# Hybrid-mixer decoder on one core: dense row products joined from 256 to 512 weight columns

## The chip, the cores and the metric

The kernel runs on 1 core of one Trainium2 chip. The metric is the device time of the whole program in microseconds; three runs of the kernel before gave 2924.04, 2924.26 and 2918.29 us, median 2924.04.

## The reference, cut to what matters

Two layers, each over 16 learned tokens, 2048 prompt tokens and 8 single-token samples. Four head groups (HGRN2, gated DeltaNet, Mamba-2 SSD, retention) read columns of one input projection; their gated outputs are joined and go through the output projection.

```python
proj = einsum('btd,de->bte', rms_norm(h, norm_w[l]), w_in[l])      # D_MODEL 1024 -> 4108 columns
...
s_ret, o_d = run_mixer(chunk_scalar_decay, step_scalar_decay,
    (rotary(to_heads(d_q, 4), pos), rotary(to_heads(d_k, 4), pos) * QK_SCALE, to_heads(d_v, 4), ret_g), s_ret, prompt)
y_d = group_norm(from_heads(o_d), ret_norm_w_l, ret_norm_b_l, 4) * silu(d_z)
y = concatenate([y_a, y_b, y_c, y_d], -1)
h = h + einsum('bte,ed->btd', y, w_out[l])                          # 1024 -> 1024
```

The retention queries d_q and keys d_k are 256 columns each, and stand next to each other in w_in (D_Q = 3084, D_K = 3340). Everything is float32.

## The kernel before, in words

**Tokens.** There are NT = 17 tiles: tile 0 has 40 rows (16 of padding, 16 learned tokens, 8 samples), the others 128 prompt tokens each. Two tiles make a block, and the first block has three (tiles 0, 1, 2); 8 blocks in all.

**Dense products in two parts.** Activations and weights are split into a high and a low fp32r part, and a product is the sum of three matmuls: high by high, high by low, low by high. There are two forms. `dense_cm` (L473 to L475) keeps weights stationary and streams a block's tokens, for a channel-major result. `dense_rows` (L483 to L485) keeps a tile's 128 (or 40) tokens stationary and streams weight columns, for a token-major result: for each of 8 slices d of the 1024 inputs three matmuls of 256 columns, 24 in a group that fills half a PSUM bank. The trace names what both read `xh`, `xl` (activations) and `wh`, `wl` (weights); the result is `pd`, a pool of two banks.

**Weights.** `wpiece` (L450 is its last line of work) loads 1024 numbers per partition (`wr`), casts them to the high part on ACT (L449, `wh`) and subtracts for the low part on DVE or POOL (L450, `wl`). A piece of `load_tm` is 4 slices of 256 columns, so a group of 256 columns needs 2 pieces. Parts lie in a ring of 6 slots and a second one of 2.

**Stages of a layer.** SSD, gated DeltaNet, HGRN2, retention (`mixD`), output projection (`outproj`). The recurrent walk of gated DeltaNet is cut into parts that `hook` lets out between pieces of the later stages, one for each unit of credit.

**mixD.** For each block: a group per tile for the queries, then one per tile for the keys, then values, then the gate in channel-major form. The eviction of a query or key group, `ev`, is the rotary: on DVE L1522 and L1524, L1525 read PSUM (256, 128 and 128 columns) and write `dt` tiles, L1526 adds; POOL multiplies by the decay (L1528). The `dt` tiles come from a ring of 4. After that each tile is transposed (L1544), scored (`sc<-dqk`), and its state is updated (L304).

**outproj.** For each tile: mixer rows `y` come back from DRAM as `yf` (L1604), ACT casts them to `xh` (L1606), DVE subtracts to `xl` (L1607); four groups of 256 columns follow, and each is added to the residual `hx` by DVE (L1613). In layer 0 the tile is then normalised and transposed (L507) for layer 1; in layer 1 it is normalised (L1623) and stored.

**Order.** A list scheduler with a timing model of its own lays out each engine's instructions from the traced program; on the chip each engine keeps that order. Evictions and weight loads are given priority (`early`, 3000 instructions ahead). Weight columns from the layer after are loaded by steps of a generator during the last tile of `outproj` (`between`).

Of the kernel before, what the change touches and what calls it, by code (L numbers as in the profile page):

```python
# [92 lines left out]
def body(tc, ctx, a, o, nch, depth, blks, off):  # L93
# [3 lines left out]
    BW = 296  # L97
# [35 lines left out]
    def later(f):  # L133
        """emit f after the next piece of work that is put off"""
        pend.append(f)
        while len(pend) > 1:
            pend.pop(0)()
# [7 lines left out]
    def hook(n=1):  # L145
        """the next parts of the walk that runs beside other work"""
        credit[0] += n
        while credit[0] >= 1:
            credit[0] -= 1
            if walk and next(walk[0], 0) == 0:  # L150
                walk.pop()

    @contextmanager
    def inorder(names):
        """what is emitted inside is issued after what was emitted before, on these engines"""
# [43 lines left out]
    def pair():  # L199
        """a bank per head half: row tiles of the array may not share a bank"""  # L200
        return psc.tile([128, 2, 512], F32, tag="sc", name="sc")
# [43 lines left out]
    # ---------------------------------------------------------------- constants  # L245
# [28 lines left out]
    # block-diagonal states (two heads a tile), in turns  # L274
# [4 lines left out]
    # full triangles (upper halves written), in turns; outside of their use: norm weights, retention's decay  # L279
# [8 lines left out]
    def next_state(L, m, pu, decay):  # L288
        """S = decay * S + update, block-diagonal"""
# [25 lines left out]
    # ---------------------------------------------------------------- helpers  # L315
# [4 lines left out]
    def power(dst, src, k=0):  # L320
        """src ** -0.5 (k=0) or 0.5 (k=1)"""
# [23 lines left out]
    def rms_scale(hx, R):  # L345
        """1 / rms of the rows"""
# [6 lines left out]
    # ---------------------------------------------------------------- per layer parameters  # L353
    def load_layer(l):
# [38 lines left out]
        # forget gate bounds: softmax of the logits over the depth axis, cumulative  # L393
# [34 lines left out]
    # ---------------------------------------------------------------- dense pieces  # L428
# [27 lines left out]
    def load_tm(w, cols, wide=False):  # L456
        n = sum(c[1] for c in cols)
        return [wpiece([w[512 * k:512 * k + 512, c0:c0 + cn] for c0, cn in cols], 4, n, wide) for k in range(2)]
# [20 lines left out]
    def dense_rows(ps, R, pcs, xh, xl):  # L479
        n = pcs[0][0].shape[2]  # L480
        for d in range(8):
            hi, lo = (x[:, d % 4] for x in pcs[d // 4])
# [12 lines left out]
    def xprep(L, t, hx, keep=False):  # L495
        """normalised rows of a token tile -> channel-major, in two exact parts, to DRAM or to the block's tiles"""
# [32 lines left out]
    def rowtile(b, nm):  # L529
        """token-major rows of 256 columns by tile"""  # L530
# [6 lines left out]
    def small(L, b, raw):  # L537
        """decays and step sizes from the narrow columns of a block's tiles"""
# [31 lines left out]
        # cumulative sums: ssd over the chunk, gdn over blocks of 32  # L570
# [15 lines left out]
    def group_scale(osrc, R, groups, eps):  # L586
        """rows scaled by 1 / rms of each group, in SBUF; eps: number or [R, groups]"""
# [26 lines left out]
    def finish(t, mi, osrc, R, eps, w, z, b=None):  # L614
        """group norm of the mixer rows; returns what takes them to channel-major, gate z [128, 2, R], and to DRAM"""
# [27 lines left out]
    # decode: partitions hold (head half, key), free (sample, pair, value)  # L643
# [12 lines left out]
    def dec_bcast(rows8):  # L656
        """[8, 256] rows -> [128 (hh k), (b p), 64]"""
# [8 lines left out]
    def pb(x, cols=None):  # L666
        """[128, 2, 8] channel-major sample columns -> [128, 8, 2, 64] broadcast over values"""
# [8 lines left out]
    def dec_sum(src, lhs, m):  # L676
        """sum over the key partitions"""
# [18 lines left out]
    # ---------------------------------------------------------------- HGRN2  # L696
# [4 lines left out]
    def mixA(L, W, b):  # L701
# [26 lines left out]
        for c0, Lc, tl in groups:  # L728
# [7 lines left out]
            def scores(h, w):  # L736
                """products of keys at j and queries at j + w in steps of h"""
# [127 lines left out]
    # ---------------------------------------------------------------- short convolutions  # L865
    def conv(L, ws, b, wi, key, hasb, out):
        """out: 3 tiles [128, 2, BW] (pairs of channel tiles)"""
# [53 lines left out]
    def conv_samples(L, wi, key, hasb, src, dst):  # L921
        """the taps come from the stored rows"""
# [29 lines left out]
    # ---------------------------------------------------------------- gated delta  # L952
# [17 lines left out]
    def prepB(L, bs):  # L970
        """what the blocks need before the states: inverses of the unit triangles"""
# [4 lines left out]
        # sums of squares of q per token and head  # L976
# [30 lines left out]
        def factors(j0, j1):  # L1007
            """factors of tiles j0 .. j1 from the sums of squares of their keys"""
# [21 lines left out]
        def scv(x, n0, n):  # L1030
            """blocks n0 .. n0 + n as [(block, row), head, column]"""
            return x[:, n0:n0 + n].rearrange("h n j i -> (n j) h i")

        # decay within blocks of 32
# [13 lines left out]
        def scores(b, t, pv, start):  # L1048
            """pv [rows, x, y, p, i]: keys by keys, keys by queries"""
# [45 lines left out]
        # negated inverse of the unit triangular blocks above the diagonal: even rows of a block in one partition,  # L1095
        # odd rows in another, each beside the whole block as it was
# [23 lines left out]
    def loadB(L, P, i):  # L1120
        """what a tile keeps in DRAM: q, k, v, inverses, scores; gates"""
# [9 lines left out]
        # a group's first tile may have to wait for the inverses  # L1131
# [6 lines left out]
    def keysB(L, X):  # L1138
        """a tile's operands for the walk over its blocks, in parts"""
# [15 lines left out]
        # running decay of a block, broadcast over key channels  # L1155
# [8 lines left out]
        # keys and queries of a block side by side, in turns  # L1164
# [23 lines left out]
    def stepB(L, X, bb):  # L1188
        """one block of the walk"""
# [17 lines left out]
    def walkB(L):  # L1207
        """the tiles in turn, in parts; a tile's operands are made during the one before"""
# [65 lines left out]
    def decB(L, ys, epsq):  # L1274
# [5 lines left out]
        # rows of v, keys scaled to unit length  # L1280
# [505 lines left out]
```

## Time and profile before

| what | value |
|---|---|
| median of 3 runs | 2924.04 us |
| lowest and highest | 2918.29 and 2924.26 us |
| span of the profiled execution | 2924.2 us |
| PE matmul, busy share of the span | 96% |
| DVE, ACT, POOL, busy share | 58%, 35%, 36% |
| mean granted TensorE clock | 0.984 |
| HBM traffic over the span | 118 GB/s |

The profiled execution's own time is its span, 2924.2 us, which is within 0.2 us of the median of the runs. Busy times of PE overlap, since matmuls are pipelined: one of 256 columns is listed with nearly 0.3 us, though the next starts far earlier. So the pace of a run of matmuls is read from the starts in the timeline, not from the mean of a group. A source line in the tables is a line of the kernel before. An idle time in brackets, with an arrow, is what the engine waited before that instruction and for whom.

### The profile page before, as it was taken

Reading aid. Unit: us, or ns where it says so; the run is one execution under the profiler, and the core shown is the slowest. Engines: PE = TensorE matmul, PEld = TensorE weight load, DVE = VectorE, ACT = ScalarE, POOL = GpSimd, SP = SyncE. Lnnn points to the kernel's source line nnn. Section 1 sums busy time; section 2 is a strip of 40 time slices with the busy share of each in tenths; the row PEclk is TensorE's granted clock in tenths of the full one; section 3 lists DMA queues with packets and bytes.
Section 4 is the critical chain, followed back from the end, with each engine's and each line's share of the span. In section 5 each row is a group of like instructions: output and inputs, shape, how many; then the busy total and the mean of one; then the engine's idle time right before and its main releaser. Section 6 shows DMA issues by size and latency. Waiting matters only on the chain.

```text
span 2924.2 us, 76217 instructions
## 1 busy us (share of the span) xinstructions
PE 2811.0 (96%) x31196; PEld 2631.0 (90%) x31196; DVE 1694.9 (58%) x4822; ACT 1010.7 (35%) x2547; POOL 1045.4 (36%) x2000
## 2 busy tenths in 40 slices
PE   6989999999999999999999999899999999999998
PEld 6889898988888899999999999888988888999998
DVE  6777765646566745364456767565556657445433
ACT  5545522333333412232244454133333333222221
POOL 4453555665232211110033543745742222112000
PEclk9999999999999999999999999999999999999999
DMA  7243364462231432247762433645432222331433
GB/s 181 68 151 118 127 163 122 133 188 76 63 112 60 129 95 88 74 128 212 215 204 93 127 106 103 152 128 152 139 101 69 78 99 83 96 116 63 134 131 109
DMA packets 391332, 349.92 MB, mean 120 GB/s; under 512 B 144312, under 2 KB 361904, under 8 KB 380744
## 3 DMA queue, kind: packets, MB, share of 16 engines
q1 hardware_dynamic: 387464, 335.96, 37.5%
q0 software_dynamic: 3520, 9.09, 1.5%
q8 instruction: 247, 4.05, 0.6%
q14 instruction: 101, 0.83, 0.1%
HBM read 247.06 MB, written 98.10 MB: 118 GB/s over the span
## 4 chain that ended last, share of the span: by engine, by line
PE 84%; DVE 6%; DMA 4%; POOL 3%; ACT 2%; issue 2%; SPq 0%; POOLq 0%; ACTq 0%; DVEq 0%
PE pd L473 10%; PE pd L474 10%; PE pd L483 10%; PE pd L484 10%; PE pd L475 10%; PE pd L485 10%; PE tr L235 7%; PE sc L235 5%; PE wo L235 5%; PE o L235 3%; DMA wr<-in_w_in_dram 1%; PE tr L611 1%; PE tr L507 1%; DVE hx L502 1%; POOL bR L1110 1%
## 5 line engine op out<-in xcount | busy, mean ns | idle before, releaser
L473 PE MATMUL pd<-xh,wh 128*128 128x256 f32 (+1 forms) x2816 | 832.1, 296 | 12.6 <-DVE hB L901 3.3
L474 PE MATMUL pd<-xl,wh 128*128 128x256 f32 (+1 forms) x2816 | 817.9, 290 | 0.0
L475 PE MATMUL pd<-xh,wl 128*128 128x256 f32 (+1 forms) x2816 | 814.1, 289 | 0.0
L483 PE MATMUL pd<-wh,xh 128*128 128x256 f32 (+3 forms) x2448 | 702.0, 287 | 6.4 <-DVE sraw L1342 4.6
L484 PE MATMUL pd<-wl,xh 128*128 128x256 f32 (+3 forms) x2448 | 700.8, 286 | 2.5 <-POOL wl L450 2.5
L485 PE MATMUL pd<-wh,xl 128*128 128x256 f32 (+3 forms) x2448 | 698.0, 285 | 0.2
L473 PEld LDWEIGHTS pd<-xh,wh 128*128 128x128 f32 x2816 | 543.9, 193 | 37.2 <-issue 16.8
L474 PEld LDWEIGHTS pd<-xl,wh 128*128 128x128 f32 x2816 | 543.8, 193 | 9.1 <-issue 6.6
L475 PEld LDWEIGHTS pd<-xh,wl 128*128 128x128 f32 x2816 | 543.6, 193 | 4.1 <-issue 2.6
L483 PEld LDWEIGHTS pd<-wh,xh 128*128 128x128 f32 (+1 forms) x2448 | 455.7, 186 | 12.6 <-issue 5.4
L484 PEld LDWEIGHTS pd<-wl,xh 128*128 128x128 f32 (+1 forms) x2448 | 455.8, 186 | 9.0 <-issue 3.4
L485 PEld LDWEIGHTS pd<-wh,xl 128*128 128x128 f32 (+1 forms) x2448 | 455.7, 186 | 4.4 <-issue 2.1
L304 DVE TENSOR_TENSOR sbd<-low,tr 64x128 f32<-64x128 f32 x384 | 109.0, 284 | 131.8 <-PE tr L235 113.4
L600 POOL TENSOR_SCALAR fm<-fm 128x4 f32<-128x4 f32 (+3 forms) x102 | 23.7, 233 | 419.2 <-DVE fm L597 393.1
L1613 DVE TENSOR_TENSOR hx<-hx,pd 128x256 f32<-128x256 f32 (+1 forms) x136 | 57.1, 420 | 175.5 <-PE pd L485 175.2
L327 POOL TENSOR_TENSOR fm<-fm,expo 128x4 f32<-128x4 f32 (+3 forms) x136 | 129.3, 951 | 49.0 <-DVE fm L602 38.7
L331 POOL TENSOR_SCALAR rm<-rm 128x1 f32<-128x1 f32 (+1 forms) x51 | 13.7, 269 | 367.2 <-ACT junk L349 366.3
L520 ACT ACTIVATE th<-pd 128x256 f32<-128x256 f32 (+2 forms) x162 | 62.3, 384 | 231.8 <-PE pd L475 194.9
L235 PEld LDWEIGHTS sc<-aq,ak 64*32 64x32 f32 (+1 forms) x7008 | 97.0, 108 | 39.7 <-issue 16.9
L235 PE MATMUL sc<-aq,ak 64*32 64x32 f32 (+1 forms) x7008 | 129.1, 200 | 2.5 <-ACT sq L773 2.0
L1110 POOL TENSOR_TENSOR bR<-bR,bW 128x120 f32<-128x120 f32 (+14 forms) x300 | 119.6, 399 | 21.6
L1109 POOL TENSOR_TENSOR bW<-bU,bR 128x120 f32<-128x120 f32 (+14 forms) x300 | 112.6, 375 | 36.4 <-DMA bR<-bscr 15.4
(519 smaller groups left out, 4989.0 us busy)
## 6 DMA issues: line engine op xcount, KB each, us to landing
xh<-xh SPq DMA_DIRECT2D x56, 1024.0 KB
xl<-xl SPq DMA_DIRECT2D x56, 1024.0 KB
wr<-in_w_in_dram SPq DMA_DIRECT2D x64, 512.0 KB
hx<-in_x_prompt_dram SPq DMA_DIRECT2D x32, 512.0 KB
y<-y SPq DMA_DIRECT2D x128, 128.0 KB
yf<-y SPq DMA_DIRECT2D x32, 512.0 KB
bld<-qkv SPq DMA_DIRECT2D x32, 384.0 KB
xh<-xh SPq DMA_DIRECT2D x8, 1184.0 KB
```

The lines of the kernel that those rows point to most:

```text
L235: T.matmul(out, l, r, start=start, stop=stop, skip_group_check=True)
L304: tt(new[rr, :, hh], low[rr, :, hh], pv, ALU.add)
L327: G.tensor_tensor(dst, src, e.broadcast_to(list(src.shape)), ALU.pow)
L473: T.matmul(ps, hi[:, d], b.xh[:, d, 0:b.n], start=(d == 0), stop=False)
L474: T.matmul(ps, hi[:, d], b.xl[:, d, 0:b.n], start=False, stop=False)
L475: T.matmul(ps, lo[:, d], b.xh[:, d, 0:b.n], start=False, stop=(d == 7))
L483: T.matmul(ps[0:R, 0:n], xh[:, d], hi, start=(d == 0), stop=False)
L484: T.matmul(ps[0:R, 0:n], xh[:, d], lo, start=False, stop=False)
L485: T.matmul(ps[0:R, 0:n], xl[:, d], hi, start=False, stop=(d == 7))
L520: act(th[0:R, 0:n], ps, AF.Tanh, scale=0.5)
L1109: f(wv, bcm(U_[0:2 * nu, j, j + 1:32], 1, m), bcl(R_[0:2 * nu, 0:m, j], 31 - j), ALU.mult)
L1110: f(R_[0:2 * nu, 0:m, j + 1:32], R_[0:2 * nu, 0:m, j + 1:32], wv, ALU.subtract)
```

## The change

Query and key columns of retention become one group of 512 columns per tile, and the output projection has two groups of 512 columns per tile in the place of four of 256. `load_tm` makes pieces of 2 slices by 512 columns (still 1024 numbers per partition), so a group needs 4 pieces and the number of pieces stays. The rotary runs over the two halves of the joined group. `hook` is called once with two units of credit, where it was called twice with one. The generator of the next layer's weights is advanced twice after each of two groups, where it was once after each of four.

```diff
     def load_tm(w, cols, wide=False):
         n = sum(c[1] for c in cols)
-        return [wpiece([w[512 * k:512 * k + 512, c0:c0 + cn] for c0, cn in cols], 4, n, wide) for k in range(2)]
+        nd = 2 if n == 512 else 4
+        r = 128 * nd
+        return [wpiece([w[r * k:r * k + r, c0:c0 + cn] for c0, cn in cols], nd, n, wide and k < 2) for k in range(8 // nd)]
...
     def dense_rows(ps, R, pcs, xh, xl):
-        n = pcs[0][0].shape[2]
+        nd, n = pcs[0][0].shape[1:3]
         for d in range(8):
-            hi, lo = (x[:, d % 4] for x in pcs[d // 4])
+            hi, lo = (x[:, d % nd] for x in pcs[d // nd])
...
     def weightsD(w):
-        return ([load_tm(w, [(c, 256)]) for c in (D_Q, D_K, D_V)], [load_cm(w, D_Z + 128 * p, True) for p in range(2)])
+        return ([load_tm(w, [(D_Q, 512)]), load_tm(w, [(D_V, 256)])], [load_cm(w, D_Z + 128 * p, True) for p in range(2)])
...
-        for x in range(2):
-            def ev(t, ps):
-                R = rows(t)
-                rp = L.rope[0:R, t - 1] if t else rope0[0:R]
-                cs, sn = rp[:, 0:32], rp[:, 32:64]
+        def ev(t, ps2):
+            R = rows(t)
+            rp = L.rope[0:R, t - 1] if t else rope0[0:R]
+            cs, sn = rp[:, 0:32], rp[:, 32:64]
+            for x in range(2):
+                ps = ps2[:, 256 * x:256 * x + 256]
...
-            dense_tm(W[0][x], b, ev)
-            hook(rD)
-        dense_tm(W[0][2], b, lambda t, ps: S.copy(v[t][0:rows(t)], ps))
+        dense_tm(W[0][0], b, ev)
+        hook(2 * rD)
+        dense_tm(W[0][1], b, lambda t, ps: S.copy(v[t][0:rows(t)], ps))
...
-        for qd in range(4):
+        for qd in range(2):
             ps = dense_rows(ptile(pd, "pd"), R, W[qd], yh[:, :, 0:R], yl[:, :, 0:R])
-            cs = slice(256 * qd, 256 * qd + 256)
+            cs = slice(512 * qd, 512 * qd + 512)
             tt(hx[0:R, cs], hx[0:R, cs], ps, ALU.add)
             if between:
                 with early():
+                    next(between)
                     Wn = next(between)
...
-            W = [load_tm(a["w_out"][l], [(256 * qd, 256)], qd == 0) for qd in range(4)]
+            W = [load_tm(a["w_out"][l], [(512 * qd, 512)], qd == 0) for qd in range(2)]
```

PE has 24096 matmuls before and 21648 with the change. On every engine the order is the same up to the first group of retention queries in layer 0, and again from the start of layer 1 up to its first group of retention queries; between those points the scheduler has laid it out anew. Counted in PE's order from there, dense matmuls stand in 174 unbroken runs before and in 135 with the change (retention and output projection of layer 0: 71 and 33, then 56 and 18; of layer 1: 68 and 2, then 59 and 2).

PE, output projection of layer 0 in its steady part, around the transposes (`tr<-ident,hx`) of one tile's normalised rows; before:

```order
L484 MATMUL pd<-wl,xh 128x256
L507 MATMUL tr<-ident,hx 128x128 x4
L485 MATMUL pd<-wh,xl 128x256
L483 MATMUL pd<-wh,xh 128x256
L507 MATMUL tr<-ident,hx 128x128 x4
L484 MATMUL pd<-wl,xh 128x256
```

and with the change:

```order
L485 MATMUL pd<-wh,xh 128x512
L486 MATMUL pd<-wl,xh 128x512
L487 MATMUL pd<-wh,xl 128x512
L509 MATMUL tr<-ident,hx 128x128 x8
L485 MATMUL pd<-wh,xh 128x512
L486 MATMUL pd<-wl,xh 128x512
L487 MATMUL pd<-wh,xl 128x512
```

The eight transposes of a tile stand together, where two dense matmuls stood between the fours; and each dense matmul has twice the columns.

DVE, retention of layer 0, around the rotary of two groups (`dt<-pd,rope` reads PSUM); before:

```order
L1522 TENSOR_TENSOR dt_15590<-pd,rope 128x256
L1524 SCALAR_TENSOR_TENSOR dt_15591<-pd,rope 128x4x32
L1525 TENSOR_TENSOR dt_15591<-pd,rope 128x4x32
L1526 TENSOR_TENSOR dt_15590<-dt_15590,dt_15591 128x256
L1556 TENSOR_TENSOR css<-sc,sq_114 128x2x2x128
L304 TENSOR_TENSOR sbd_110<-low,tr 64x2x64 x2
L620 TENSOR_REDUCE fm<-o 128x4
L621 TENSOR_SCALAR fm<-fm 128x4
L623 TENSOR_TENSOR xc<-o,fm 128x256
L1522 TENSOR_TENSOR dt_15622<-pd,rope 128x256
```

and with the change:

```order
L1525 TENSOR_TENSOR dt_15522<-pd,rope 128x256
L1527 SCALAR_TENSOR_TENSOR dt_15523<-pd,rope 128x4x32
L1528 TENSOR_TENSOR dt_15523<-pd,rope 128x4x32
L1525 TENSOR_TENSOR dt_15529<-pd,rope 128x256
L1527 SCALAR_TENSOR_TENSOR dt_15530<-pd,rope 128x4x32
L1528 TENSOR_TENSOR dt_15530<-pd,rope 128x4x32
L1529 TENSOR_TENSOR dt_15522<-dt_15522,dt_15523 128x256
L1529 TENSOR_TENSOR dt_15529<-dt_15529,dt_15530 128x256
L1559 TENSOR_TENSOR css<-sc,sq_115 32x2x2x32
```

The eight operations of a tile's query and key halves stand back to back, six readers of PSUM first; the scores' masking (`css`) and the state (`sbd`) come behind all of them, where they stood between two groups of four.

## Rows read from the trace of the kernel before

**Rows 1.** The page: busy times, and shares of the chain that ended last.

```profile
PE 2811.0 (96%) x31196; PEld 2631.0 (90%) x31196; DVE 1694.9 (58%) x4822; ACT 1010.7 (35%) x2547; POOL 1045.4 (36%) x2000
...
PE 84%; DVE 6%; DMA 4%; POOL 3%; ACT 2%; issue 2%; SPq 0%; POOLq 0%; ACTq 0%; DVEq 0%
```

**Rows 2.** Windows: us; busy us (count) of PE, PEld, DVE, ACT, POOL; clock; DMA.

```profile
1012.00:1276.00 264.00, 262.18 (x2593) 248.55 (x2591) 131.73 (x380) 64.85 (x158) 47.88 (x85) 1.00 0.27 87
1276.00:1488.00 212.00, 212.00 (x1795) 210.92 (x1794) 95.36 (x166) 56.67 (x91) 23.56 (x42) 1.00 0.69 208
2490.00:2735.00 245.00, 243.28 (x2123) 231.89 (x2122) 120.13 (x330) 64.07 (x149) 42.96 (x67) 1.00 0.30 97
2735.00:2918.00 183.00, 181.53 (x1521) 181.33 (x1519) 64.57 (x99) 32.60 (x48) 12.93 (x32) 1.00 0.37 125
```

**Rows 3.** Line L483 of dense_rows: count, duration ns (min/median/max), first and last start, forms.

```profile
L483 PE MATMUL pd<-wh,xh x2448: 274/283/573, 14.8 to 2916.0; 128*128 128x256 f32 x157, 128*128 128x268 f32 x19, 128*40 128x256 f32 x11, 128*40 128x268 f32 x2
```

**Rows 4.** PE timeline (start us, us, line): runs of 256 columns, output projection, then retention.

```profile
2799.74 0.28 PE L484 MATMUL pd<-wl,xh 128*128 128x256 f32 x1
...
2823.14 0.28 PE L485 MATMUL pd<-wh,xl 128*128 128x256 f32 x1
...
1104.64 0.28 PE L485 MATMUL pd<-wh,xl 128*128 128x256 f32 x1
...
1106.53 0.28 PE L483 MATMUL pd<-wh,xh 128*128 128x256 f32 x1
```

**Rows 5.** PE timeline, a run of 296 columns in retention: first and last.

```profile
1051.81 0.30 PE L474 MATMUL pd<-xl,wh 128*128 128x296 f32 x1
...
1054.79 0.30 PE L475 MATMUL pd<-xh,wl 128*128 128x296 f32 x1
```

**Rows 6.** The 512-column fp32r matmul of the SSD stage: its durations, then its neighbours.

```profile
L235 PE MATMUL sc<-cgu,l128r x68: 242/397/796, 52.2 to 1772.2; 128*128 128x512 f32 x64, 32*32 32x128 f32 x4
...
247.33 0.39 PE L235 MATMUL sc<-cgu,l128r 128*128 128x512 f32 x1
247.57 0.28 PE L473 MATMUL pd<-xh,wh 128*128 128x256 f32 x1
247.68 0.28 PE L474 MATMUL pd<-xl,wh 128*128 128x256 f32 x1
```

**Rows 7.** PE timeline, retention: dense matmuls behind a tile's transposes.

```profile
1100.14 0.36 PE L484 MATMUL pd<-wl,xh 128*128 128x256 f32 x1
1100.34 0.28 PE L485 MATMUL pd<-wh,xl 128*128 128x256 f32 x1
```

**Rows 8.** DVE timeline: a rotary's readers of PSUM; a 512-column read of PSUM.

```profile
1096.18 0.42 DVE L1522 TENSOR_TENSOR dt<-pd,rope 128x256 f32<-128x256 f32 x1 [0.56 <-PE pd L485]
1096.52 0.28 DVE L1524 SCALAR_TENSOR_TENSOR dt<-pd,rope 128x128 f32<-128x128 f32 x1
1096.72 0.28 DVE L1525 TENSOR_TENSOR dt<-pd,rope 128x128 f32<-128x128 f32 x1
...
1491.37 0.69 DVE L513 TENSOR_TENSOR xtl<-tr,xth 128x512 fp32r<-128x512 f32 x1 [1.41 <-ACT xth L512]
```

**Rows 9.** The last eviction; line L1606, the cast of mixer rows, and whom it waited for.

```profile
2916.57 0.42 DVE L1613 TENSOR_TENSOR hx<-hx,pd 128x256 f32<-128x256 f32 x1 [2.46 <-PE pd L485]
...
L1606 ACT CAST xh<-yf x34: 447/1048/1055, 1273.1 to 2893.6; 128x1024 fp32r<-128x1024 f32 x32, 128x320 fp32r<-128x320 f32 x2
...
  PE pd L484: 175.2, 28
```

**Rows 10.** Start of retention, layer 0: the last low part of its weights, its first matmul.

```profile
1004.56 1.23 DVE L450 TENSOR_TENSOR wl<-wr,wh 128x1024 fp32r<-128x1024 f32 x1
...
1012.28 0.31 PE L483 MATMUL pd<-wh,xh 128*40 128x256 f32 x1
```

**Rows 11.** Loads of stationary operands on L484: count, busy us, mean ns.

```profile
L484 PEld LDWEIGHTS pd<-wl,xh 128*128 128x128 f32 x2304 | 439.1, 191 | 5.3 <-issue 3.4
```

## The prediction

> **What bounds the kernel now.** I read the page first: PE is busy 96% of the span and carries 84% of the chain that ended last, DVE only 6% [rows 1]. That is an average over unlike stages, so I cut out the four stretches that the change touches, retention and output projection of each layer, 904 us together. PE is busy 262.2 of 264, 212.0 of 212, 243.3 of 245 and 181.5 of 183 us there, at a granted clock of 1.00 (the 2.4 GHz level), while DVE fills about half or less [rows 2]. So in these stretches every nanosecond that PE's queue gets shorter should come off the end, as long as nobody makes PE wait. What counts is PE's pace from start to start; the listed 283 ns of one matmul [rows 3] overlap with its neighbours.
>
> **The pace of 256 columns.** In the output projection, 197 dense matmuls start between 2799.74 and 2823.14 us: 23.40 / 196 = 119.4 ns each. In a run of 17 in retention it is 1.89 / 16 = 118.1 ns [rows 4]. At 2.4 GHz 256 columns stream in 106.7 ns, so 11 to 13 ns of each step are not columns. Whether these are paid per matmul or per column decides the change, because it halves the matmuls and leaves the columns as they are.
>
> **The price of 512 columns.** Rows nearest in kind, three readings:
> - A run of 23 matmuls with 296 columns takes 2.98 / 22 = 135.5 ns each [rows 5]. 40 columns more than in the same stage's 118.1 ns cost 17.4, or 0.43 ns a column; 256 more columns make 118.1 + 111 = 229.
> - The SSD stage has a 512-column fp32r matmul with a 128x128 stationary operand. Its median duration is 397 ns against 283, so 114 ns more [rows 3, 6]: 119.4 + 114 = 233.
> - Behind it the dense matmul after next starts 0.35 us after it (247.33 to 247.68) [rows 6]; less one step of 119 that is 231, read to 10 ns. The step itself shows as 0.24 and the one behind as 0.11, so part of the long step is handed back.
> The lower bound is the pace of 256 plus the bare streaming of 256 more columns, 119.4 + 106.7 = 226. The upper one is 233. I take 228, nearer the lower end, since the durations include a pipeline's latency that the pace does not.
>
> **The change, part by part.**
> - Output projection. 17 tiles x 4 groups x 24 matmuls x 2 layers = 3264 become 1632. Each pair costs 2 x 119.4 = 238.8 and becomes 228: 1632 x 10.8 ns = **17.6 us** (between 1632 x 5.8 = 9.5 and 1632 x 12.8 = 20.9).
> - Retention queries with keys. 17 x 2 x 24 x 2 = 1632 become 816: 816 x (236.2 - 228) = **6.7 us** (2.6 to 8.3).
> - Returns to dense work. The step after the first dense matmul that follows transposes is 0.20 us, not 0.12 [rows 7], so 0.08 us is lost at each return. The scheduler's new order has 135 unbroken dense runs for 174: 39 x 0.08 = **3.1 us** (0 to 4, as not every return costs this).
> - Evictions. The residual add reads 512 columns at once: 0.69 us by the other 512-column read of PSUM, for two of 0.42 [rows 8, 9]. DVE gains; on the path only the last one counts, which is longer by **0.27 us**. Everything behind it (normalisation, store) already needed the whole row.
> - Rotary. The six readers of a joined bank take about 2 x 0.82 = 1.6 us (starts 0.34 and 0.20 apart, the last 0.28 long) [rows 8], and a bank is wanted again only after the next group, 24 x 228 = 5.5 us. Two banks of 512 columns hold twice the work that they did, so I cost this at nothing. The cover is those 4 us; without it each of the 34 joined groups would wait.
> - Weights. A first group now needs four pieces, not two. In retention the last low part starts at 1004.56 and takes 1.23 us, and the first matmul starts at 1012.28 [rows 10], so nothing waits. In the output projection four pieces feed 24 x 228 = 5.5 us of work, as they fed 48 x 119.4 = 5.7 before. The loads, their bytes and SP's order there are nearly as they were. Nothing.
> - Prefetch of a tile's mixer rows: its cast waited for PE to release the old operand 28 times of 34 [rows 9], not for a DMA, so a tile that is half a microsecond shorter does not run dry. Nothing.
> - Credit of the walk and order of the next layer's loads: the same sums, moved by one group. Nothing, with some 2 us either way where layer 1 begins.
> Sum: 17.6 + 6.7 + 3.1 - 0.3 = 27.1 us. The profiled execution took 2924.2 and the median of runs is 2924.04, so both give **2897**.
>
> **A rule against it.** The steps of 118 to 119 ns carry 11 to 13 ns beyond the columns [rows 4], and I book most of that per matmul. The Trainium skill, in "TensorE: Matmul & The Clock Gate", section "Back-to-back issue gap", gives an isolated gap of columns / 2.4 plus 2.5 ns, which is 109.2 and 215.8 ns: joining would return 2.5 ns, and the estimate by that formula is 2448 x 2.5 = 6 us, or 2918. The trace does not agree with its price for 256 columns.
>
> **Rivals.**
> - *The excess grows with the columns.* Then 512 columns cost what two matmuls of 256 do, 236 to 239 ns; only the returns to dense work help, and the time is 2924.2 - 3.1 + 0.3 = 2921. For it: the long step of 0.24 us [rows 6]. Against it: the step behind is short, and 296 columns would cost 118.1 x 296 / 256 = 136.6, where 135.5 is read [rows 5]; that alone is a thin margin. The formula of the page named above would end near here too.
> - *The stationary load hides.* A load is listed with 191 ns [rows 11], longer than a step of 119 but shorter than one of 228. If the excess is a load that does not quite fit, a long stream covers it, and 512 columns cost the bare 213 ns: 1632 x 25.8 + 816 x 23.2 = 61 us, with the returns 64, and the time is 2860. Against it: the 512-column rows that exist are not that fast [rows 6], though short steps stand around them. The same section of the skill gives 131 ns for sustained matmuls of 512 columns, by which the estimate would be some 2660; a stream of 213 ns excludes that here.
> - *DVE's block holds up retention.* Eight rotary operations stand back to back, and the state and the score mask wait behind them. If a tile's scores or state then reach PE 1.5 us late with no dense work laid out in between, PE stands still 34 x 1.5 = 51 us and the end is 2948. It decides from 27 / 34 = 0.8 us a tile. For it: the order of DVE. Against it: DVE is half idle there and PE had under 2 us of idle time in each retention stretch [rows 2], with a group of 5.5 us between most dependent steps.
> - *The change does not reach the chain.* In the output projection of layer 0 the DMA engines are at 0.69 [rows 2]; if they set the pace as soon as PE is quicker, that stretch keeps its time and 8.8 us are lost: 2906. Against it: PE had no idle time there.
>
> **How the numbers follow.** My forecast has 0.74, the growing excess 0.09, the hidden load 0.07, DVE's block 0.05, the DMA limit 0.05. Runs of this kernel spread over 6 us, and about 0.2% (5.8 us) is what a measurement can tell from no change. My own terms give 2924.2 - 33 = 2891 at best and 2924.2 - 12 = 2912 at worst, the DMA limit lies inside, and with 3 to 5 us for the spread the range is 2886 to 2915. It leaves out the growing excess, the hidden load and DVE's block, 0.21, of which the nearer part of the first falls within it. Faster by over 0.2%: 0.74 + 0.07 + 0.05 = 0.86; the same: 0.09; slower: 0.05.
>
> **What would show it.** In the profile after: starts of the 512-column dense matmuls 226 to 230 ns apart; the output projection of layer 1 shorter by about 9 us, that of layer 0 by a little more, each retention stretch by 3 to 5; PE's idle time in the four stretches still a few us; everything up to 1012 us as it was, and layer 1 up to its retention shifted as a whole. Steps of 236 or more would make the price wrong; steps near 228 with long waits of PE for `sbd`, `css` or `pd` would make the cover wrong.

## Result and the profile after

The changed kernel takes **2904.13 us** (median of 6 runs, 2900.61 to 2908.91), the kernel before, run beside it, 2924.15 (6 runs, 2912.96 to 2926.84). The ratio is 0.994 with an interval of 0.9923 to 0.9957: faster by 20 us, where 27 were forecast. The profiled execution took 2902.62 us, its span is 2900.7. (Times are some 1.8 us longer than spans in these runs, so the 2924.2 of the kernel before, from which the prediction starts, is a span and not that execution's time.)

First the page of the changed kernel: busy time of PE and PEld, then the lines of `dense_rows` and the residual add. PE's own busy time fell by 27.2 us [rows 1], more than the end did.

```profile
PE 2783.8 (96%) x28748; PEld 2488.9 (86%) x28748; DVE 1684.7 (58%) x4754; ACT 1011.6 (35%) x2547; POOL 1048.0 (36%) x2000
...
L485 PE MATMUL pd<-wh,xh 128*128 128x512 f32 (+5 forms) x1632 | 561.9, 345 | 7.9 <-DVE sraw L1344 5.0
L486 PE MATMUL pd<-wl,xh 128*128 128x512 f32 (+5 forms) x1632 | 558.7, 342 | 5.0 <-POOL wl L450 5.0
L487 PE MATMUL pd<-wh,xl 128*128 128x512 f32 (+5 forms) x1632 | 557.6, 342 | 0.0
...
L1616 DVE TENSOR_TENSOR hx<-hx,pd 128x512 f32<-128x512 f32 (+1 forms) x68 | 46.6, 685 | 122.3 <-PE pd L487 122.3
```

Then the pace, from starts on PE's timeline of the changed kernel: a run in layer 1's output projection, and one in layer 0's retention.

```profile
2790.00 0.39 PE L485 MATMUL pd<-wh,xh 128*128 128x512 f32 x1
...
2794.08 0.39 PE L485 MATMUL pd<-wh,xh 128*128 128x512 f32 x1
...
1089.07 0.39 PE L487 MATMUL pd<-wh,xl 128*128 128x512 f32 x1
...
1091.38 0.39 PE L485 MATMUL pd<-wh,xh 128*128 128x512 f32 x1
```

The first run has 18 steps, 4.08 / 18 = 227 ns; the second has 10, 231 ns. Two steps of 256 columns cost 238.8 [rows 4].

For the whole time the span is cut at named matmuls, the same in both kernels: retention of layer 0, its output projection, the **start of layer 1** (from the first 268-column row matmul of layer 1 to its first 512-column `cgu` matmul), the rest of its SSD stage up to the last of these, DeltaNet, HGRN2, retention, output projection. In layer 1 retention begins at 2455.0 us and the output projection at 2714.9, so the windows of [rows 2] start 35 and 20 us late there. Windows of the kernel before (columns as in [rows 2]):

```profile
1012.28:1273.57 261.29, 259.97 (x2575) 247.26 (x2574) 129.07 (x374) 62.59 (x154) 47.88 (x85) 1.00 0.27 86
1273.57:1488.26 214.69, 214.19 (x1811) 212.36 (x1812) 97.84 (x172) 58.65 (x95) 23.56 (x42) 1.00 0.69 208
1488.26:1528.22 39.96, 35.12 (x245) 33.73 (x242) 25.12 (x68) 20.79 (x52) 17.88 (x15) 0.91 0.66 187
1528.22:1772.16 243.94, 237.40 (x1915) 228.97 (x1914) 173.77 (x488) 117.55 (x307) 115.52 (x152) 0.99 0.34 107
1772.16:2070.66 298.50, 278.26 (x3115) 259.38 (x3114) 174.75 (x530) 95.20 (x254) 161.51 (x317) 0.95 0.50 140
2070.66:2455.03 384.37, 377.25 (x5950) 333.39 (x5947) 237.06 (x753) 142.37 (x395) 144.30 (x363) 0.99 0.31 94
2455.03:2714.92 259.89, 258.66 (x2576) 246.63 (x2575) 128.41 (x373) 62.66 (x154) 48.65 (x85) 1.00 0.26 86
2714.92:2924.22 209.30, 201.12 (x1690) 199.46 (x1690) 78.42 (x128) 39.80 (x63) 16.92 (x40) 0.99 0.36 122
```

The same windows of the changed kernel:

```profile
1010.15:1267.43 257.28, 255.57 (x2167) 222.72 (x2166) 131.63 (x377) 63.46 (x155) 50.31 (x87) 1.00 0.27 86
1267.43:1475.62 208.19, 207.15 (x995) 166.83 (x995) 88.08 (x134) 55.47 (x91) 19.55 (x37) 1.00 0.67 208
1475.62:1529.82 54.20, 39.17 (x243) 37.39 (x242) 29.77 (x79) 24.59 (x62) 21.16 (x18) 0.81 0.60 163
1529.82:1769.34 239.52, 236.00 (x1915) 227.68 (x1914) 165.45 (x474) 115.31 (x299) 114.46 (x150) 1.00 0.34 109
1769.34:2061.34 292.00, 275.48 (x3114) 256.68 (x3113) 177.10 (x533) 95.54 (x256) 162.71 (x320) 0.96 0.50 144
2061.34:2442.17 380.83, 374.77 (x5950) 331.49 (x5947) 236.73 (x753) 142.39 (x395) 144.53 (x363) 1.00 0.32 95
2442.17:2700.23 258.06, 256.41 (x2168) 223.41 (x2167) 130.26 (x372) 62.57 (x154) 49.17 (x85) 1.00 0.27 86
2700.23:2900.65 200.42, 192.47 (x877) 154.80 (x875) 74.69 (x95) 41.04 (x63) 16.92 (x40) 0.99 0.37 127
```

With the lengths, the first number behind each window, a reader can do the balance. The four joined stretches (the first two and the last two) give 4.0 + 6.5 + 1.8 + 8.9 = **21.2 us**. The start of layer 1, where nothing is joined, takes **14.2 us more**. The three stages behind it, in which every engine has the order of before, take 4.4 + 6.5 + 3.5 = **14.4 us less**. So the total looks like the joined stretches alone, while two large shifts elsewhere cancel. The experiments ask what each of the three is.

### The profile page after: what moved, and what is told of

The parts are those of the page before. It is cut to its first block, busy times and chain, and to the rows that moved or that the text cites. A ratio compares the mean times of both kernels' runs of the same rounds, so it can differ in the third digit from the quotient of the medians.

```text
span 2900.7 us, 71224 instructions
## 1 busy us (share of the span) xinstructions
PE 2783.8 (96%) x28748; PEld 2488.9 (86%) x28748; DVE 1684.7 (58%) x4754; ACT 1011.6 (35%) x2547; POOL 1048.0 (36%) x2000
## 5 line engine op out<-in xcount | busy, mean ns | idle before, releaser
L485 PE MATMUL pd<-wh,xh 128*128 128x512 f32 (+5 forms) x1632 | 561.9, 345 | 7.9 <-DVE sraw L1344 5.0
L486 PE MATMUL pd<-wl,xh 128*128 128x512 f32 (+5 forms) x1632 | 558.7, 342 | 5.0 <-POOL wl L450 5.0
L487 PE MATMUL pd<-wh,xl 128*128 128x512 f32 (+5 forms) x1632 | 557.6, 342 | 0.0
L485 PEld LDWEIGHTS pd<-wh,xh 128*128 128x128 f32 (+1 forms) x1632 | 302.7, 185 | 49.8 <-issue 6.7
L486 PEld LDWEIGHTS pd<-wl,xh 128*128 128x128 f32 (+1 forms) x1632 | 302.9, 186 | 44.5 <-POOL wl L450 5.4
L487 PEld LDWEIGHTS pd<-wh,xl 128*128 128x128 f32 (+1 forms) x1632 | 302.5, 185 | 37.9 <-issue 1.2
L327 POOL TENSOR_TENSOR fm<-fm,expo 128x4 f32<-128x4 f32 (+3 forms) x136 | 129.8, 954 | 52.3 <-DVE fm L604 42.1
L1616 DVE TENSOR_TENSOR hx<-hx,pd 128x512 f32<-128x512 f32 (+1 forms) x68 | 46.6, 685 | 122.3 <-PE pd L487 122.3
```

The lines of the kernel that those rows point to most:

```text
L327: G.tensor_tensor(dst, src, e.broadcast_to(list(src.shape)), ALU.pow)
L485: T.matmul(ps[0:R, 0:n], xh[:, d], hi, start=(d == 0), stop=False)
L486: T.matmul(ps[0:R, 0:n], xh[:, d], lo, start=False, stop=False)
L487: T.matmul(ps[0:R, 0:n], xl[:, d], hi, start=False, stop=(d == 7))
```

## Experiments

Letters in the expectations: theory A, each matmul carries a fixed part of some 12 ns beside its columns; B, the gain is one of fewer, larger groups and of their order; C, SP's order at the start of layer 1 (the loads `dgb`) costs the lead that layer 0 won; D, late weights cost it.

### One join at a time

Output projection alone: retention keeps three groups of 256 columns, with the rotary and `hook` as in the kernel before.

```
-        return ([load_tm(w, [(D_Q, 512)]), load_tm(w, [(D_V, 256)])], ...
+        return ([load_tm(w, [(c, 256)]) for c in (D_Q, D_K, D_V)], ...
...
```

> Only the output projection is joined; retention is as before. Theory A (each matmul carries some 12 ns that are not columns, so a joined pair gives back about 11): 1632 matmuls fewer, both output projections shorter by 6 to 9 us, both retention stretches within 1.5 us of the kernel before, time 2906 to 2913. Theory B (the gain comes from fewer, larger groups: evictions, returns to dense work and the order around them, not from the matmuls): most of those effects are in retention, so this version should keep less than a third of the 20 us, 2918 or more.

Measured: 2908.33 us (2907.08 to 2916.49), ratio 0.9964 [0.995, 0.9978]. Output projections -4.4 and -8.6 us, start of layer 1 +12.6.

Retention alone: the output projection keeps four groups of 256.

```
-        for qd in range(2):
+        for qd in range(4):
...
-            W = [load_tm(a["w_out"][l], [(512 * qd, 512)], qd == 0) for qd in range(2)]
+            W = [load_tm(a["w_out"][l], [(256 * qd, 256)], qd == 0) for qd in range(4)]
```

> Only retention is joined; the output projection is as before. Theory A: 816 matmuls fewer at steps of 230 to 231 ns for two of 118, so 4 to 5 us in both retention stretches together and nothing elsewhere: 2918 to 2921. Theory B: half of the gain or more, 2914 or less.

Measured: 2903.34 us (2897.84 to 2906.78), ratio 0.9941 [0.9928, 0.9955]. Retention -4.0 and -1.8 us, to the tenth what it gives in the changed kernel; start of layer 1 +2.2. The whole gain is there again with a quarter of what the joined stretches give, because DeltaNet is 9.5 us shorter and HGRN2 4.1. So the loss at the start goes with layer 0's joined output projection, and much of the gain in the end does not come from joined matmuls.

### The price of a matmul

The joined groups, with each matmul issued as two of 256 columns.

```
+            step = 256 if n == 512 else n
+            for x, y, k in ((xh, hi, 0), (xh, lo, 1), (xl, hi, 2)):
+                for c in range(0, n, step):
+                    T.matmul(ps[0:R, c:c + step], x[:, d], y[:, c:c + step], ...
```

> The changed kernel with its joined groups, pieces of weights and evictions, but each matmul of 512 columns issued as two of 256, with a stationary load each. Theory A: steps of 118 to 120 ns again, the four stretches back to within 3 us of the kernel before each, time 2919 to 2926. Theory B: steps of 118 to 120 ns too, but the gain stays: 2908 or less.

Measured: 2905.43 us (2902.61 to 2907.22), ratio 0.9949 [0.9936, 0.9962]. In the four stretches the gain is gone (-0.4, +3.3, +0.9, -0.9 us), as A has it; the total kept 15 us all the same and was misjudged. In layer 1 the start is 4.2 us shorter than in the kernel before, the rest of the SSD stage 5.6, DeltaNet 8.7 and HGRN2 4.6.

Then the same with `step = 128`.

> The changed kernel with every 512-column row matmul issued as four of 128 columns into the same PSUM rows, order of groups untouched. Theory A (each matmul carries a fixed part of some 12 ns beside its columns at 2.4 GHz): a step of 128 columns lasts 53.3 + 12 = 65 to 66 ns, four of them 262 ns against 228 for the 512, so each of the two output projections (816 such matmuls) grows by 816 x 34 ns = 28 us, to 236 us in layer 0 (after: 208.2) and 228 us in layer 1 (after: 200.4). Rival 1 (the gain of the change was one of order and waits; the price is by column alone): the stages stay within 3 us of the changed kernel's. Rival 2 (a short matmul can't hide the load of its stationary operand): steps of 100 ns and more, the stages grow by 816 x 172 ns = 140 us each.

Measured: 3383.67 us; the output projections grew to 373.2 and 367.8 us. PE's timeline of this kernel (one row for four matmuls), first with the 128 tokens of a full tile as stationary operand, then with the 40 of the first tile:

```profile
1400.10 0.61 PE L488 MATMUL pd<-wh,xh 128*128 128x128 f32 x4
...
1401.89 0.61 PE L488 MATMUL pd<-wl,xh 128*128 128x128 f32 x4
...
1352.88 0.41 PE L488 MATMUL pd<-wl,xh 128*40 128x128 f32 x4
...
1354.33 0.40 PE L488 MATMUL pd<-wl,xh 128*40 128x128 f32 x4
```

1.79 / 16 = 112 ns with 128 stationary columns, 1.45 / 24 = 60 with 40. Theory A said 66 and falls for short matmuls; rival 2, that a short matmul does not hide its load, holds. The kernel before has a matmul that streams almost nothing, two columns behind a load of 128 (operands in plain fp32):

```profile
408.31 0.95 PE L235 MATMUL tr<-hones,bsq 128*128 128x2 f32 x8
```

The median step inside its runs is 112 ns as well, from the same trace; with 40 and 32 stationary columns such steps take 38 to 39 and 31 to 32 ns at the short end. So it is the load that sets them. The same tile in the changed kernel (512 columns) and in the kernel before (256 columns):

```profile
1280.07 0.40 PE L487 MATMUL pd<-wh,xl 128*40 128x512 f32 x1
...
1282.41 0.40 PE L485 MATMUL pd<-wh,xh 128*40 128x512 f32 x1
```

```profile
1276.83 0.28 PE L483 MATMUL pd<-wh,xh 128*40 128x256 f32 x1
...
1277.65 0.28 PE L484 MATMUL pd<-wl,xh 128*40 128x256 f32 x1
```

2.34 / 10 = 234 ns and 0.82 / 7 = 117: with 40 stationary columns two of 256 cost what one of 512 does. That asked for a last run: layer 0's output projection in groups of 256 columns and layer 1's in groups of 512, both with 64 tokens of each tile. It leaves out the other rows, which keep the layer's input.

```
-            ps = dense_rows(ptile(pd, "pd"), R, W[qd], yh[:, :, 0:R], yl[:, :, 0:R])
+            H = min(R, 64)
+            ps = dense_rows(ptile(pd, "pd"), H, W[qd], yh[:, :, 0:H], yl[:, :, 0:H])
...
+            tt(hx[0:H, cs], hx[0:H, cs], ps, ALU.add)
...
```

> The kernel with layer 0's output projection in groups of 256 columns and layer 1's in groups of 512, but both compute 64 token rows of each tile in place of 128 (the other rows keep the input of the layer), so every row matmul there has a stationary operand of 64 columns. Theory L (what a joined matmul saves is bound to a stationary operand of 128 columns: with the 40 columns of the first tile, steps are 60, 117 and 233 ns for 128, 256 and 512 columns, so nearly in proportion, and with 128 columns 111, 119.5 and 227): with 64 columns a step of 256 lasts 117 ns and one of 512 233, so joining would be worth 1 ns of 234 and no 11. Theory A (each matmul carries its 12 ns whatever its stationary operand, and the first tile's steps are only disturbed by what runs beside it): 119 to 120 and 227 to 228 ns, as with 128 rows.

Measured: 2884.49 us, with half of the rows left out. PE's timeline of this kernel, layer 0 and layer 1:

```profile
1400.50 0.28 PE L485 MATMUL pd<-wh,xh 128*64 128x256 f32 x1
...
1402.44 0.28 PE L487 MATMUL pd<-wh,xl 128*64 128x256 f32 x1
...
2790.41 0.39 PE L485 MATMUL pd<-wh,xh 128*64 128x512 f32 x1
...
2793.86 0.40 PE L485 MATMUL pd<-wh,xh 128*64 128x512 f32 x1
```

1.94 / 17 = 114 ns and 3.45 / 15 = 230. Two of 256 are 228, so joining is worth nothing (it loses 2 ns), as theory L has it, with 114 where it said 117. **What a join saves here hangs on a stationary operand of 128 columns**: there the step of 256 is 119.4 ns, 5 more than with 64, while 512 columns hide the load (227, and 230 with 64). The Trainium skill, "TensorE: Matmul & The Clock Gate", section "LDWEIGHTS (loading the stationary operand)", says that a load takes as long as its columns divided by 1.2, in ns; by that figure the estimate is 107 for 128 columns and 33 for 40. The traces agree to 5 or 6 ns where next to nothing is streamed, with 112 and 38 to 39, though the profile lists a 128-column load with 191 ns [rows 11].

### How far stages repeat

The kernel before and the changed kernel were profiled a second time, with nothing edited.

> The kernel before, unchanged, profiled a second time: how far do the stages of layer 1 whose instruction order the change leaves alone (from the first 512-column cgu matmul to the start of retention) repeat? Theory R (they ran 14 us shorter in the changed kernel because of what the change does ahead of them): the second profile shows again 243 to 245 us for the rest of the SSD stage, 297 to 300 us from its end to HGRN2, 383 to 386 us for HGRN2. Theory S (they scatter from one execution to the next, with the waits on DMA and the stretches at half clock): at least one of the three lies 4 us or more from the first profile, and the sum of the three moves by 5 us or more.

> The changed kernel, unchanged, profiled a second time. Theory R (its 6.5 us less in layer 1's DeltaNet stage and 3.5 us less in HGRN2, at an instruction order equal to that of before, repeat, since before's two profiles gave 298.5 and 299.2, 384.4 and 384.2 us): 290 to 294 us and 379 to 382 us again, and the start of layer 1 at 52 to 56 us. Theory S (that was one execution's luck): at least one of these two stages comes within 2 us of before's.

Measured: spans 2920.5 and 2900.5 us. In us, first and second profile:

| stretch of layer 1 | before | after |
|---|---|---|
| start | 40.0, 42.0 | 54.2, 52.5 |
| rest of SSD | 243.9, 238.9 | 239.5, 239.9 |
| DeltaNet | 298.5, 299.2 | 292.0, 290.9 |
| HGRN2 | 384.4, 384.2 | 380.8, 384.4 |

Both theories are right in part. The rest of the SSD stage and HGRN2 scatter by 4 to 5 us from one execution to the next (theory S). The longer start and the shorter DeltaNet stage repeat (theory R): on the means, start and rest of SSD together lose 10.7 us (282.4 to 293.1), and DeltaNet gives back 7.4. Some 3 us of such a shift may be scatter: layer 0's DeltaNet stage, up to whose end the two kernels have one order, took 290.4 and 290.8 us before and 287.5 twice after, and with that order it took 287.0 to 290.4 in the other kernels of the study.

### The start of layer 1

Who PE waited for in it, in the kernel before:

```profile
PE tr L507 <- DVE hx L502: 2.8, 1, 2.8
PE pd L484 <- POOL wl L450: 1.0, 1, 1.0
PE sc L235 <- POOL cgu L1353: 1.0, 1, 1.0
```

and in the changed kernel:

```profile
PE sc L235 <- POOL cgu L1355: 7.1, 2, 6.8
PE pd L475 <- ACT u L889: 4.1, 2, 3.2
PE pd L486 <- POOL wl L450: 2.6, 1, 2.6
PE pd L485 <- ACT wh L449: 1.2, 1, 1.2
```

`cgu` shares its buffers with the tiles `xth` and `xtl`, from which SP stores a token tile's normalised rows. The changed kernel's SP queue, then its POOL, which waited 9.64 us for such a store:

```profile
1503.93 7.46 SPq L1294 DMA_DIRECT2D dgb<-smd  x5
1511.44 2.40 SPq L517 DMA_DIRECT2D xh<-xth  x1
1513.94 2.15 SPq L517 DMA_DIRECT2D xl<-xtl  x1
1516.18 2.91 SPq L517 DMA_DIRECT2D xh<-xth  x1
...
1522.86 0.31 POOL L1355 TENSOR_SCALAR_AFFINE_SELECT cgu<-gh 32x128 fp32r<-32x128 f32 x1 [9.64 <-DMA xh<-xth]
```

Five of the eight broadcast loads of the decode gates stand ahead of the last tile's four stores and hold SP for 7.46 us; a sixth stands ahead of the fourth store. In the kernel before the only one is that ahead of the fourth:

```profile
1514.37 0.38 SPq L515 DMA_DIRECT2D xh<-xth  x1
1515.39 0.61 SPq L515 DMA_DIRECT2D xl<-xtl  x1
1516.10 0.46 SPq L515 DMA_DIRECT2D xh<-xth  x1
1516.61 1.21 SPq L1292 DMA_DIRECT2D dgb<-smd  x1
```

Of the 14.2 us, 10.2 are idle time of PE (54.20 - 39.17 for 39.96 - 35.12), and 4.0 are longer busy time. With PE's waits go stretches at the lower granted clock: the mean of the window is 0.81, before 0.91. With levels of 1.2 and 2.4 GHz that is 54.2 x 2 x 0.19 = 21 us at the lower one, against 40.0 x 2 x 0.09 = 7.

First all `dgb` loads were put behind SP's earlier work, in both layers:

```
+        with inorder((ET.SP,)):
             for x, cc in ((0, 4), (1, 12)):
...
```

> The changed kernel, with the eight small loads of the decode step's gates (dgb) put behind what SP was given before them in the program. In the changed kernel five of them stand ahead of the last tile's four stores at the start of layer 1, and the 12.6 us by which layer 0 ended earlier were gone by 1530 us. Theory C (SP's order there holds back the slots of those stores, then POOL's cgu, then PE): the wait of 6.8 us of PE for cgu goes, layer 1's SSD stage starts 6 us or more earlier against the changed kernel, time 2894 to 2900. Theory D (the lead is lost because the next layer's weights come late, whatever SP does with these loads): no more than 2 us, 2901 to 2906.

Measured: 2908.99 us (2903.82 to 2915.56), ratio 0.9961 [0.9948, 0.9975]. The start of layer 1 fell to 44.1 us, as C has it, but layer 0, whose order moved too, lost 4.6 us in its SSD stage and 7.4 in DeltaNet against the kernel before, and the time met neither range. So the edit was confined to layer 1 (`inorder((ET.SP,) if L.l else ())`):

> The changed kernel, with the eight dgb loads of layer 1 alone put behind SP's earlier work, so that the last tile's xh and xl stores no longer stand behind them; layer 0 as in the changed kernel. Theory C (the start of layer 1's SSD stage lost its lead to SP's order): that stretch falls from 54 to 42 to 45 us with about one stretch of half clock in place of six, the time to 2893 to 2896 us. Rival (what is won there is given back, since the gates now come late and the decode step of layer 1 moves in the DeltaNet stage): the stretch falls as well, but the DeltaNet stage grows by 6 to 10 us, and the time stays within 3 us of 2904.

> The changed kernel with layer 1's dgb loads put late, profiled a second time, since the first profile fell on an execution 16 us above this kernel's median. Theory C: the start of layer 1's SSD stage lasts 42 to 45 us (the changed kernel: 54.2), the output projection of layer 0 again 208 us, and what is left of the 10 us in the end is 4 to 8 us, a time of 2896 to 2900 us. Rival (late gates only move the wait): the start stays over 50 us, or the DeltaNet stage of layer 1 lasts 300 us again, some 8 us more than the changed kernel's.

Measured: 2899.68 us (2894.63 to 2917.32), ratio 0.9941 [0.9925, 0.9956]. The two profiled executions show 45.7 and 45.2 us for the start and no wait for `cgu`. Layer 0's output projection, meant to stay, takes 213.2 and 211.1 us (the changed kernel: 208.2 and 207.8), and DeltaNet takes 300.2 and 296.2 (292.0 and 290.9), with new waits of PE of 5.1 and 5.3 us for POOL's `bgx`. So C is right on most of what lengthens the start, and the rival on the total: most of it is given back, the ratio is that of the changed kernel, and the median lies between the two ranges.

Then layer 0's last tile alone went back to four groups of 256 columns, which leaves three `dgb` loads ahead of the stores:

```
+        if between:
+            W = [[[x[:, :, c:c + 256] for x in pc] for pc in w] for w in W for c in (0, 256)]
-        for qd in range(2):
+        for qd in range(len(W)):
...
-                    next(between)
                     Wn = next(between)
```

> The changed kernel, but the output projection of layer 0's last tile alone reads the joined weights in four groups of 256 columns, with one piece of layer 1's first weights asked for behind each, as before; the other sixteen tiles and layer 1 stay joined. On SP three dgb loads stand ahead of the last xh store (changed kernel: five, before and the kernel with retention alone: one). Theory C (the joined groups of this one tile put the gate loads ahead of the stores that layer 1's SSD stage waits for): the start of layer 1 lies between before's and the changed kernel's, 45 to 49 us for 54.2 and 52.5, layer 0's output projection at 208.5 us, the time at 2894 to 2900 us. Rival 1 (the lead itself is the cause: SP has less time for the same work, whatever the order): the start stays at 52 to 55 us, the time at 2902 to 2905 us. Rival 2 (the first stage waits for nothing but what the SSD weights bring, asked for in lumps of two): the start falls to 40 to 42 us, the time to 2890 to 2894 us.

Measured: 2901.72 us (2900.82 to 2909.39), ratio 0.994 [0.9921, 0.9958]; start 49.9 us, wait for `cgu` 4.8. By the number of `dgb` loads ahead of the last of the four stores, 0, 1, 3 and 6 (late gates, before, this kernel, the changed one), PE waited for `cgu` 0, 1.0, 4.8 and 7.1 us and the start took 45.2, 40.0, 49.9 and 54.2. The wait follows the count. The start follows it in the other kernels too: with one load it took 42.2 (retention alone), 42.1 (the next section) and 40.6 (64 tokens), with five 52.6 (output projection alone), and 35.7 with none in the kernel with matmuls cut to 256 columns. The late gates alone do not fit, with none and 45.2: waits for ACT's `u` (5.0 us) and for weight parts of POOL and ACT (4.5) stay there, and these runs don't separate their causes. The start missed its range by 1 us and the total by 2; layer 0's output projection came to 212.2 and not 208.5.

That the lead as such is not the cause shows in the kernel with 64 tokens: its layer 0 has the output projection of before in groups of 256 and is as short as the changed kernel's (208.1 us), yet with one load ahead of the last store the start takes 40.6.

### Joined where it pays

Retention joined in both layers, the output projection in layer 1 alone.

```
...
+            k = 4 if l == 0 else 2
+            W = [load_tm(a["w_out"][l], [(1024 // k * qd, 1024 // k)], qd == 0) for qd in range(k)]
```

> Retention joined in both layers, the output projection in layer 1 alone (layer 0's stays at four groups of 256). Theory C (the joined output projection of layer 0 gains 6 us and, through the order in which the start of layer 1 is then issued, loses 12): layer 1's start stays near 42 us as with retention alone, its output projection keeps the 8.7 us, so 2903.3 - 8 = 2895 us. Rival (the times of the unchanged stages make up for whatever lead comes into layer 1): 2903 +- 3 us. Rival 2 (the price per matmul is all there is): 8 us of 27 less gained than with both layers joined, 2910 to 2913 us.

Measured: **2896.36 us** (2894.04 to 2900.42) beside 2918.21 for before, ratio 0.9928 [0.9914, 0.9942]. Start 42.1 us, DeltaNet 287.4, layer 1's output projection 200.4: all of layer 1's gain, with a start as long as before (40.0 and 42.0). This is the lowest median of the study for the whole computation, 7 us below retention alone (4 by the ratios), in the sense of C. Its interval overlaps that of the changed kernel, so that it beats the full change is likely and not shown.

### Why DeltaNet is shorter at an equal order

The waits of PE in layer 1's DeltaNet stage that differ, before and after:

```profile
PE tr L1146 <- DMA bld<-qkv: 10.9, 2, 6.5
```

```profile
PE tr L1148 <- DMA bld<-qkv: 7.2, 2, 6.5
```

The second of the two waits, 4.3 us (4.1 in the second profile), is 0.8 after (none in the second): some 4 of the 7.4 us. The rest is mostly shorter busy time, 277.9 to 275.0 us on the means, whose cause was not followed. At that load both queues issue at once; the kernel before, then the changed one:

```profile
1961.71 0.64 POOL L1103 DMA_DIRECT2D bU<-bscr  x1 [2.82 <-DMA bscr<-bdc]
...
1961.93 2.27 SPq L1130 DMA_DIRECT2D bld<-qkv  x2
```

```profile
1957.94 1.22 SPq L1132 DMA_DIRECT2D bld<-qkv  x2
...
1958.28 0.64 POOL L1105 DMA_DIRECT2D bU<-bscr  x1 [3.36 <-DMA bscr<-bdc]
```

Before, POOL's gather is issued 0.2 us ahead of the loads and their issue takes 2.27 us; after, 0.3 us behind, and it takes 1.22. The second profiles have the same two orders (0.2 us ahead; 1.4 behind). In the nine other profiles (all but that of `step = 128`) the gather is issued 1.1 to 1.9 us behind the loads, and the second wait is at most 0.9. That a fraction of a microsecond between two queues decides this wait fits all these traces, but it was not tried by itself: a kernel that moves these loads moves other work too. It does not set the stage's length alone, since DeltaNet took 296 us and more with the gates late.

## Why the prediction came out as it did

PE's time in the four stretches, by start-to-start steps of the two first profiles:

| us | forecast | measured |
|---|---|---|
| row products, output projections, with 15 of the 39 returns | -17.6 - 1.2 = -18.8 | -8.5 - 8.8 = -17.3 |
| row products, retention, with 24 returns | -6.7 - 1.9 = -8.6 | -5.3 - 2.5 = -7.8 |
| other work of PE in these stretches (no term) | 0 | +3.9 |
| last eviction and tail | +0.3 | +0.3 |
| start of layer 1 and rest of its SSD stage | 0 (2 either way) | +9.8 |
| layer 1's DeltaNet and HGRN2 | 0 | -10.0 |
| all before 1010 us | 0 | -2.1 |
| sum | -27.1 | -23.5 |

(Row products were 198.0 and 195.6 us in the two output projections before and 189.5 and 186.8 after. The tail, from the last eviction to the end 7.65 us before and 7.91 after, lies inside the other work and is left out of the measured sum, which is that of the two spans. By the medians of runs it is -20.)

- **The price.** 228 ns was right: 227 in the output projections, 231 in retention. The output projections were met to 1.5 us, returns included. Its reason was right for this shape and wrong as a rule: the prediction put the 11 to 13 ns beyond the columns down to each matmul. With 64 stationary columns 512 columns cost a little more than twice what 256 do (230 for 2 x 114), so there the excess grows with the columns, as that rival has it. The 5 ns more that a matmul of 256 columns takes with a load of 128 are what a join saves, once for each of the two. The rival of the hidden load named the right resource, and only its size was wrong: long streams reach 227 and not the 213 that it counted on. The 40-row tiles gain nothing. The rule that was weighed there (the Trainium skill, "TensorE: Matmul & The Clock Gate", section "Back-to-back issue gap": 2.5 ns per matmul beside its columns) agrees with neither case: a join returned 11.8 ns with 128 stationary columns and -2 with 64.
- **Returns to dense work** came near their price. By the starts in the traces, the first steps of unbroken runs of dense matmuls exceed the median step by 13.9 us in all before (171 runs) and by 11.3 after (134): 2.6 us for 3.1, and the second profiles give the same two sums.
- **Other work** has no term in the prediction. The transposes and state products of retention take 2.0 us more in the two layers, so of 7.8 us 5.8 reach the end of these stretches, and not "3 to 5" in each but 4.0 and 1.8. In layer 0's output projection other work grew from 16.7 to 18.7 us, so of 8.5 us 6.5 reach the end of the stretch, where a little more than 9 was named.
- **Rotary, weights, prefetch** at nothing: PE's idle time in the four stretches is 4.4 us after, 3.5 before. DVE's block did not come, and neither did the DMA limit, at 0.67 of the DMA engines.
- **Credit and order of the next layer's loads** is the step that failed: "nothing, with some 2 us either way where layer 1 begins". Start and rest of the SSD stage lost 10.7 us on the means of two profiles. Most of it goes with the order of eight small loads on SP against the last tile's stores, and with the lower granted clock that stands beside PE's waits: with these loads late the start fell by 7.9 us (means of 53.4 and 45.5), though layer 0's output projection grew by 3 to 5. The remaining 4.5 us over the 41.0 of before stay open. The prediction looked at SP's order in the output projection and found it nearly as it was; it had no term for the stores at the seam of the layers.
- **"Layer 1 up to its retention shifted as a whole"** was wrong as well. DeltaNet repeats 7.4 us shorter. That, which nobody forecast, made up for most of the loss at the start, so the time came out near what the joined stretches give alone (21.2 us) by luck.

## What to carry to other kernels

Price a longer matmul by its stationary operand too: joining two of 256 columns paid some 11 ns with 128 stationary columns and nothing with 64 or 40. Where an edit lets the order change, read the queue of each DMA issuer around the next stage's first stores, not only PE's rows: here the start of the next layer lost half of what was won, most of it with that order. And balance a result by stretches, with a second profile of each kernel: a total near the forecast hid two shifts, of 10.7 and 7.4 us on the means, that nearly cancelled.

## What was not expected of the hardware

- A 128-column matmul took 112 ns with 128 stationary columns and 60 with 40; the joined products cut into such pieces made the whole kernel 16% longer than before (3383.67 us for 2918.21).
- With 128 stationary columns a step took 112 ns whether 2 or 128 columns were streamed.
- At 512 columns the wider stationary operand was not slower: 227 ns with 128 columns, 230 with 64, 234 with 40.
- One broadcast load of `dgb` held SP's queue for 1.5 us on the mean of five (7.46 in all; 0.62 for one in the kernel with retention alone), where a store of a tile's rows took 0.4 when nothing crowded it.
- Stages with the same order on every engine differed by 5 us between two executions, and by 7 us, repeatably, between two kernels that differ only ahead of them.
